# Order of loads and of work at the start of a two-layer decoder kernel

## The chip, the core and the metric

The kernel runs on one core of one Trainium2 chip, as a single launch. TensorE (PE) multiplies, VectorE (DVE), ScalarE (ACT) and GpSimd (POOL) do the element-wise work, and SyncE (SP) only issues transfers between the chip's memory and the on-chip buffers. Each engine takes its own instructions strictly in order and waits on semaphores for the others. The metric is device time in microseconds (us) of one execution; lower is better.

## The reference

Two layers on a sequence of 1024 rows of 1024 numbers. What matters here is how a layer begins:

```python
cos, sin = rope_tables(positions)          # once, used by both layers
cond = jax.nn.silu(c)
# in each layer:
mod = cond @ w_ada + b_ada
shift, scale, gate = jnp.split(mod, 3, axis=-1)
h = layer_norm(x) * (1.0 + scale[:, None, :]) + shift[:, None, :]
proj = h @ w_in
u, v, z_a, q, k, val, z_b, q_idx, k_idx, w_idx = jnp.split(proj, SPLIT_POINTS, axis=-1)
k = apply_rope(k, cos, sin); k_idx = apply_rope(k_idx, cos, sin)
q_idx = apply_rope(q_idx, cq, sq)          # 8 index heads; then scores, top-k, attention
```

Nothing of `h` exists before the shift and scale of its channels do, so at the start of layer 0 the 8 MB of `w_ada` for shift and scale, the rows `x` and the key weights all have to arrive before the first projections can end. Layer 1 finds its own modulation computed during layer 0.

## The kernel before

Rows are tiled by 128 (8 blocks), channels by 128 (8 groups, `NK`), the sequence in two halves of 512 columns. All matrix products are made of three matmuls (high by high, high by low part, low by high), so each weight tile and each column of `h` is split in two: ScalarE rounds the high part, GpSimd or VectorE subtracts the low one (`split`, L310).

`head` (L819) does layer 0's start. It issues the loads in the order of its loop: `x` blocks at positions `XK`, the key weights (`load_kv`) at position `H0`, the rotary tables at `RT`, and 16 pairs of `w_ada` tiles (8 channel groups for each of two column halves c; a pair holds shift and scale columns, tile name `h`). `ada_cols` (L857) forms shift with TensorE (matmul into `po`) and scale with VectorE (a chain of 8 multiply-adds into `ga`), turns both into columns with small matmuls, and VectorE writes four channels of shift and scale to `modT` (L876). The modulated, transposed rows are built by `hT` (L268): TensorE transposes a block of 128 channels (L281), ScalarE scales and shifts it out of PSUM (L288, tile `gc` or `gb`), VectorE casts the high part (L292), and VectorE or GpSimd subtracts the low one (L295, tile `h`). `project_k` (L355) issues the matmuls (L358) into `pacc`.

The order of the work around the change: `head` returns after the first half's key projections and after both halves of `h`; `layer` then alternates between the keys (`kv`, L381) and the first pair of index queries (`queries`, L416). So TensorE's program order is keys of half 0, index queries of half 0, keys of half 1, index queries of half 1, then the second pair of index queries, which is the first work on weights loaded by `layer` itself. Keys share their two PSUM banks (`acc`) with the queries. The rotary tables go through a table in the chip's memory: `rope_tables` (L144) computes four pieces of 32 rows, writes them (L168), and `load_tables` (L170) reads them back four times over, at the start of each layer.

The instruction order inside an engine is not the source order: a list scheduler of the compiler (`schedule_with_timeline_sim=True`) orders each engine's queue by its own estimate of when things are ready. `issue_after` keeps an instruction behind a marked one. SP's queue carries all transfers. Three loads put single 4-byte elements into a column per partition: the condition `c` (L116), the bias of `w_ada` (L180) and `v_norm_g` (L468).

Of the kernel before, what the change touches and what calls it, by code (L numbers as in the profile page):

```python
# [66 lines left out]
class Trunk:  # L67
# [44 lines left out]
    def consts(self):  # L112
        nc, a = self.nc, self.a
        self.cond = self.col("cond", 1, NK)
        cT = self.col("cT", 1, NK)
# [4 lines left out]
        make_identity(nc, self.ident)  # L120
        self.mhalf = self.col("mhalf", 1)
# [14 lines left out]
        self.cs_dram = dram("cs_tab", [2, 32, S])  # L136
# [7 lines left out]
    def rope_tables(self):  # L144
        nc, a = self.nc, self.a
        W = S // 4
        nc.sync.dma_start(self.invf, a["inv_freq"])
        nc.sync.dma_start(self.ztab, a["ztab"][:, 0:36].rearrange("p (k g) -> p k g", k=6))
        nc.sync.dma_start(self.iota8, a["ztab"][:, 36:44])
        pi = self.g("ga", dt=I32)[:, :W]  # L150
        for c in range(4):
            nc.sync.dma_start(pi[c * 32:(c + 1) * 32], a["positions"][0, c * W:(c + 1) * W].partition_broadcast(32))
        ang, kk = self.g("ga")[:, :W], self.g("ga")[:, :W]
        nc.vector.tensor_copy(ang, pi)
        nc.vector.tensor_scalar(ang, ang, self.invf[:, 0:1], None, op0=ALU.mult)
        nc.vector.tensor_scalar(kk, ang, 1.0 / TWO_PI, MAGIC, op0=ALU.mult, op1=ALU.add)
        nc.vector.tensor_scalar(kk, kk, MAGIC, None, op0=ALU.subtract)
        for part in two_pi_parts():
            nc.vector.scalar_tensor_tensor(ang, kk, -part, ang, op0=ALU.mult, op1=ALU.add)
        nc.vector.tensor_scalar(ang, ang, 3.1415925, -3.1415925, op0=ALU.min, op1=ALU.max)  # L160
        sin, cos = self.g("ga")[:, :W], self.g("ga")[:, :W]
        nc.scalar.activation(sin, ang, AF.Sin)
        nc.scalar.activation(cos, ang, AF.Sin, scale=0.5)
        nc.vector.tensor_tensor(cos, cos, cos, op=ALU.mult)
        nc.vector.tensor_scalar(cos, cos, -2.0, 1.0, op0=ALU.mult, op1=ALU.add)
        for w, tab in enumerate((cos, sin)):
            for c in range(4):
                nc.sync.dma_start(self.cs_dram[w][:, c * W:(c + 1) * W], tab[c * 32:(c + 1) * 32])  # L168

    def load_tables(self):  # L170
        self.cos, self.sin = self.u("r"), self.u("r")
        for w, tab in enumerate((self.cos, self.sin)):
            for c in range(4):
                self.nc.sync.dma_start(tab[c * 32:(c + 1) * 32], self.cs_dram[w])


    def ada_begin(self, l):
        self.mod[l] = self.col("modT", 2, 2 * NK)
        bT = self.col("badaT", 2, 2 * NK)
# [74 lines left out]
    NORM = 2  # L254
# [47 lines left out]
    XT = ('r', 'r', 'q', 'q')  # L302
# [33 lines left out]
    def load_kv(self, l):  # L336
# [4 lines left out]
        nc.sync.dma_start(r2, w_in[l, :, C_KI:C_KI + 72].rearrange("(k p) c -> p k c", p=P))  # L341
        hi = [self.u("w", (P, NK, P), F32R) for _ in range(2)]
# [4 lines left out]
        return hi, lo  # L347

# [32 lines left out]
    def kv(self, l, wts, ready=None):  # L381
# [73 lines left out]
    def sgu_setup(self, l):  # L455
# [11 lines left out]
        self.vg = self.col("vg", 1, 4)  # L467
        nc.sync.dma_start(self.vg, a["v_norm_g"][l].rearrange("(j p) -> p j", p=P), allow_slow_non_contiguous=True)  # L468
# [338 lines left out]
    def run(self):  # L807
# [8 lines left out]
        for l in range(DEPTH):  # L816
            wts = self.layer(l, wts if l else self.head())

    def head(self):  # L819
        nc = self.nc  # L820
        xs, raw = [], ([], [])
        for n in range(2 * NK + 1):
            for _ in range(self.XK.count(n)):
                xs.append(self.load_row(self.xin[0], len(xs), ("q", "q", "kd", "kd")[len(xs)]))
            if n == self.H0:
                kvw = self.load_kv(0)
            if n == self.RT:
                self.rope_tables()
            if n == 1:
                self.ada_begin(0)  # L830
            if n < 2 * NK:
                c, k = divmod(n, NK)
# [7 lines left out]
        for x in xs:  # L840
            self.ln_row(x, 4)
        hT = self.hT(0, range(4), xs, *self.HK[0])
        kv = [self.p("acc") for _ in range(2)]
        for c in range(2):
            if c:
                self.ada_cols(c, raw[c])
            for k in range(4 * c, 4 * c + 4):
# [3 lines left out]
        xs = [self.ln_row(self.load_row(self.xin[0], b, self.XT[b - 4])) for b in range(4, NB)]  # L851
        if not self.QE:
            qiw = self.load_pair(0, C_QI, True, "ya")
        self.load_tables()
        self.drain(self.hT(0, range(4, NB), xs, *self.HK[1]))
        return kvw, qiw, kv

    def ada_cols(self, c, tiles):
# [3 lines left out]
        for k, w in enumerate(tiles):  # L862
# [4 lines left out]
            else:  # L867
                nc.vector.scalar_tensor_tensor(sc, w[:, 1, :], ck, sc, op0=ALU.mult, op1=ALU.add)
# [207 lines left out]
```

## Time and profile before

| what | value |
|---|---|
| median of 3 runs (lowest, highest) | 1181.41 us (1180.64, 1185.3) |
| the profiled execution: its time, its span | 1184.14 us, 1182.4 us |
| busy share of the span: PE, DVE, ACT, POOL | 94%, 71%, 43%, 49% |
| chain that ended last, by engine | PE 53%, DVE 8%, DMA 3% |
| projections (L358): matmuls, busy | 2304, 542.5 us |
| mean granted TensorE clock | 0.977 |

The profile has several views. The busy table by stretches gives for each stretch its length and for each engine (PE, its weight loads, DVE, ACT, POOL) the busy time with its number of instructions, then the granted TensorE clock (1.00 is full speed), the mean busy share of the 16 DMA engines, and the GB/s that they moved. The timeline gives start, duration, engine, source line, operation and its tiles (written<-read), how many instructions are merged, and in brackets the idle time before them with what ended it. The table of DMA issues gives the tiles, how many transfers, KB each, and the median us from issue to landing. In the rows, `SPq` is SP's queue of transfers. The first 6 us of the span have no matmul at all, and TensorE's busy share in 40 slices of 30 us starts with 5 and 8 tenths, against 9 in most others.

### The profile page before, as it was taken

Reading aid. Unit: us, or ns where it says so; the run is one execution under the profiler, and the core shown is the slowest. Engines: PE = TensorE matmul, PEld = TensorE weight load, DVE = VectorE, ACT = ScalarE, POOL = GpSimd, SP = SyncE. Lnnn points to the kernel's source line nnn. Section 1 sums busy time; section 2 is a strip of 40 time slices with the busy share of each in tenths; the row PEclk is TensorE's granted clock in tenths of the full one; section 3 lists DMA queues with packets and bytes.
Section 4 is the critical chain, followed back from the end, with each engine's and each line's share of the span. In section 5 each row is a group of like instructions: output and inputs, shape, how many; then the busy total and the mean of one; then the engine's idle time right before and its main releaser. Section 6 shows DMA issues by size and latency. Waiting matters only on the chain.

```text
span 1182.4 us, 16568 instructions
## 1 busy us (share of the span) xinstructions
PE 1109.5 (94%) x5460; PEld 883.6 (75%) x5460; DVE 838.2 (71%) x1884; ACT 512.2 (43%) x988; POOL 575.8 (49%) x485
## 2 busy tenths in 40 slices
PE   5889999999989799989988999999999989999997
PEld 0468888777768688867666788888778877787885
DVE  6775757889869356689975447579985737878775
ACT  0343555221122445466764526552222146667561
POOL 1464311566432666365766532114654457565653
PEclk9989999999989799999998999999999999999999
DMA  8935420378742664331322453213724345132311
GB/s 260 286 94 160 142 72 26 127 244 237 228 130 81 204 188 143 108 99 63 99 89 73 116 152 121 58 57 114 249 90 152 98 141 198 54 102 78 117 36 63
DMA packets 127057, 152.11 MB, mean 129 GB/s; under 512 B 17396, under 2 KB 94580, under 8 KB 126968
## 3 DMA queue, kind: packets, MB, share of 16 engines
q1 hardware_dynamic: 126968, 151.03, 40.5%
q8 instruction: 43, 0.70, 0.2%
q14 instruction: 46, 0.38, 0.1%
HBM read 111.40 MB, written 35.40 MB: 124 GB/s over the span
## 4 chain that ended last, share of the span: by engine, by line
PE 53%; DVE 8%; DMA 3%; issue 2%; POOL 2%; ACT 1%; SPq 0%; DVEq 0%; ACTq 0%; POOLq 0%
PE pacc L358 22%; PE pacc L747 14%; PE ps L685 4%; PE ppt L705 4%; PE po L711 3%; PE po L710 2%; PE ppt L535 2%; PE ps L535 1%; POOL h L732 1%; DVE ga L709 1%; DVE ya L686 1%; DVE w L686 1%; PE po L451 1%; DMA gc<-ya 1%; DVE gb L717 1%
## 5 line engine op out<-in xcount | busy, mean ns | idle before, releaser
L358 PE MATMUL pacc<-h,w 128*128 128x512 f32 (+2 forms) x2304 | 542.5, 389 | 6.9 <-ACT gc L501 6.4
L358 PEld LDWEIGHTS pacc<-h,w 128*128 128x128 f32 (+1 forms) x2304 | 420.0, 187 | 103.0 <-ACT gc L501 10.1
L312 POOL TENSOR_TENSOR w<-wr,w 128x512 fp32r<-128x512 f32 (+1 forms) x100 | 135.0, 1366 | 211.7 <-ACT w L311 203.0
L747 PE MATMUL pacc<-h,gc 128*128 128x512 f32 x768 | 199.6, 405 | 13.4 <-ACT gc L311 12.1
L747 PEld LDWEIGHTS pacc<-h,gc 128*128 128x128 f32 x768 | 145.1, 194 | 43.3 <-ACT gc L311 13.0
L542 DVE SCALAR_TENSOR_TENSOR sc<-gc,wi,sc 128x384 f32<-128x384 f32 (+3 forms) x140 | 97.4, 740 | 56.6 <-ACT gc L537 54.0
L311 ACT ACTIVATE w<-wr 128x512 fp32r<-128x512 f32 (+1 forms) x100 | 56.8, 602 | 154.4 <-PE pacc L358 95.0
L709 DVE TENSOR_TENSOR ga<-ppt,ga 128x512 fp32r<-128x512 f32 x144 | 97.0, 684 | 20.7 <-ACT ga L708 20.1
L685 PE MATMUL ps<-kd,q 128*128 128x512 f32 (+4 forms) x384 | 104.1, 368 | 7.1 <-DVE mx L686 6.5
L708 ACT ACTIVATE ga<-ppt 128x512 fp32r<-128x512 f32 x144 | 82.7, 592 | 38.6 <-PE ppt L705 37.9
L377 POOL TENSOR_TENSOR ga<-ga,ga 128x512 fp32r<-128x512 f32 (+2 forms) x40 | 52.7, 1324 | 83.6 <-ACT ga L376 80.4
L685 PEld LDWEIGHTS ps<-kd,q 128*128 128x128 f32 x384 | 64.2, 192 | 23.8 <-DVE mx L686 17.4
L694 POOL TENSOR_SCALAR w<-w,rd 128x256 f32<-128x256 f32 (+6 forms) x77 | 61.4, 801 | 40.8 <-DVE rd L693 24.4
L691 ACT ACTIVATE w<-w,mx 128x256 f32<-128x256 f32 (+6 forms) x77 | 60.6, 787 | 35.5 <-DVE mx L686 34.9
L705 PE MATMUL ppt<-ident,w 128*128 128x128 f32 x349 | 74.1, 275 | 0.5 <-POOL w L694 0.5
L248 POOL TENSOR_TENSOR rs<-rs,mhalf 128x1 f32<-128x1 f32 x48 | 30.2, 638 | 86.4 <-DVE rs L247 85.8
L710 PE MATMUL po<-ga,vv 128*128 128x512 f32 x144 | 61.9, 430 | 9.1 <-DVE gb L717 5.7
L550 DVE TENSOR_SCALAR_CACHE_REDUCE junkd<-sc,sv 128x384 int8<-128x384 f32 (+2 forms) x72 | 67.8, 942 | 1.7
L711 PE MATMUL po<-ga,vv 128*128 128x512 f32 x144 | 63.1, 438 | 4.1 <-DVE ga L709 3.9
L694 POOL TENSOR_SCALAR ya<-ya,rd 128x256 f32<-128x256 f32 (+6 forms) x51 | 40.8, 801 | 52.3 <-DVE rd L693 30.4
L537 ACT ACTIVATE gc<-ppt 128x384 f32<-128x384 f32 (+3 forms) x96 | 47.8, 526 | 40.2 <-PE ppt L535 35.8
L705 PE MATMUL ppt<-ident,ya 128*128 128x128 f32 x227 | 58.0, 275 | 1.4 <-DVE modT L235 1.4
(197 smaller groups left out, 1729.9 us busy)
## 6 DMA issues: line engine op xcount, KB each, us to landing
wr<-in_w_in SPq DMA_DIRECT2D x50, 512.0 KB, 4.4
r<-in_w_ada SPq DMA_DIRECT2D x32, 512.0 KB, 4.7
q<-q SPq DMA_DIRECT2D x112, 128.0 KB, 3.2
q<-ga SPq DMA_DIRECT2D x48, 256.0 KB, 2.2
h<-in_w_ada SPq DMA_DIRECT2D x32, 256.0 KB, 4.8
wr<-in_w_out SPq DMA_DIRECT2D x16, 512.0 KB, 4.1
r<-r SPq DMA_DIRECT2D x14, 512.0 KB, 3.6
r<-x SPq DMA_DIRECT2D x12, 512.0 KB, 4.5
```

Source lines behind the costliest of these rows:

```text
L312: self.nc.gpsimd.tensor_tensor(lo, src, hi.bitcast(F32), op=ALU.subtract)
L358: self.nc.tensor.matmul(acc[:m, :tn], w[:, k, :m], h[:, k % 2, t0:t0 + tn], start=(k == 0 and i == 0), stop=(k == NK - 1 and i == 2))
L542: nc.vector.scalar_tensor_tensor(sc[:, c0:c0 + w], r[:, :w], wsc, sc[:, c0:c0 + w], op0=ALU.mult, op1=ALU.add)
L550: self.nc.vector.tensor_scalar(j[:, :n], sc, thr, None, op0=op, op1=ALU.add, accum_out=out)
L685: self.last_pe = nc.tensor.matmul(ps[:, :w], q[:, g * 4 + h, :], self.KD[x][:, c0:c0 + w], start=(x == 0), stop=(x == 1)).ins
L694: nc.gpsimd.tensor_scalar(pm[:, :n], pm[:, :n], rd, 0.0, op0=ALU.mult, op1=ALU.add)
L705: nc.tensor.transpose(pt[:, h * P:(h + 1) * P], pr[h][:, kt * P:(kt + 1) * P], self.ident)
L708: nc.scalar.activation(ph, pt, AF.Copy)
L709: nc.vector.tensor_tensor(pl, pt, ph.bitcast(F32), op=ALU.subtract)
L710: nc.tensor.matmul(o, self.V[:, kt, :], ph, start=(kt == 0), stop=False)
L711: nc.tensor.matmul(o, self.V[:, kt, :], pl, start=False, stop=(kt == i))
L747: self.nc.tensor.matmul(acc, s[:, k, :], m[:, cs], start=(first and k == i == 0), stop=(not more and k == 3 and i == 2))
```

## The change

- `c`, the `w_ada` bias and `v_norm_g` are loaded as rows (8, 16 and 4 rows of 128) and turned into columns by one TensorE transpose each (`ada_bias` for the bias).
- SP's order at the start is fixed by the source: `c`, the bias, the eight 512 KB tiles of column half 0 (shift and scale in one transfer, 2 KB runs as before), `x` blocks 0 to 3, key weights, the eight tiles of column half 1, `x` blocks 4 to 7 (before: two of these stood behind the first table reads), the first index weights. The small inputs of the rotary tables are issued from ScalarE's queue.
- The rotary table operations on VectorE start behind the last sum of column half 0 (`mark["sum"]`), the table is written as 128 rows of 1 KB in 2 transfers instead of 8, behind the last `w_ada` load; the reads are 8 as before, in 1 KB runs instead of 4 KB.
- `NORM = 6`: the eight normalisations of layer 0's `x` blocks move from VectorE to ScalarE (L262's form), with one more small VectorE operation each.
- `head` becomes a generator: keys of half 0, then, in the same pass, `h` and keys of half 1, and only then the index queries of both halves. `load_pair` and `load_kv` are split into load and split parts.

```diff
 def consts(self):
-        nc.sync.dma_start(cT, a["c"].rearrange("o (k p) -> p (o k)", p=P), allow_slow_non_contiguous=True)
-        nc.scalar.activation(self.cond, cT, AF.Silu)
+        crow = self.g("gb", (NK, P))
+        nc.sync.dma_start(crow, a["c"].rearrange("o (k p) -> (o k) p", p=P))
...
+        nc.tensor.transpose(cT[:, :NK], crow, self.ident[:NK, :NK])
+        nc.scalar.activation(self.cond, cT[:, :NK], AF.Silu)
...
+    def rope_inputs(self):
...
+        nc.scalar.dma_start(self.invf, a["inv_freq"])
...
+    def rope_tables(self, pi, dma):
...
+        with self.behind("sum"):
+            nc.vector.tensor_copy(ang, pi)
...
-            for c in range(4):
-                nc.sync.dma_start(self.cs_dram[w][:, c * W:(c + 1) * W], tab[c * 32:(c + 1) * 32])
+            with self.tc.issue_after(dma):
+                nc.sync.dma_start(self.cs_dram[w], tab)
...
+        self.brow = self.t("brow", [2 * NK, P])
+        self.nc.sync.dma_start(self.brow, self.a["b_ada"][l, 0:2 * D].rearrange("(k p) -> k p", p=P))
+
+    def ada_bias(self, l):
...
-        self.nc.sync.dma_start(bT, self.a["b_ada"][l, 0:2 * D].rearrange("(k p) -> p k", p=P), allow_slow_non_contiguous=True)
-        self.nc.vector.tensor_scalar(bT[:, NK:], bT[:, NK:], 1.0, None, op0=ALU.add)
+        nc.tensor.transpose(pt[:, :2 * NK], self.brow, self.ident[:2 * NK, :2 * NK])
+        nc.vector.tensor_copy(self.bT[:, :NK], pt[:, :NK])
+        nc.vector.tensor_scalar(self.bT[:, NK:], pt[:, NK:2 * NK], 1.0, None, op0=ALU.add)
...
-    NORM = 2
+    NORM = 6
...
 def head(self):
+        ada_loads(0)
+        pi = self.rope_inputs()
+        xs = [self.load_row(x, b, ("q", "q", "kd", "kd")[b]) for b in range(4)]
+        kvr = self.kv_raw(0)
+        dma = ada_loads(1)
+        xs += [self.load_row(x, b, "r") for b in range(4, NB)]
+        qir = self.pair_raw(0, C_QI)
+        self.ada_bias(0)
         self.ada_cols(0, raw[0])
+        for b in range(4):
+            self.ln_row(xs[b], 4)
+        self.rope_tables(pi, dma)
+        kvw = self.kv_split(*kvr)
+        out = {}
+        for half in range(2):
+            hT = self.hT(0, range(half * 4, half * 4 + 4), xs[half * 4:half * 4 + 4], *self.HK[half])
+            kv = [self.p("acc") for _ in range(2)]
+            for k in range(NK):
+                if half == 0 and k == 4:
+                    self.ada_cols(1, raw[1])
                 next(hT)
                 for j in range(2):
-                    self.project_k(kv[j], kvw[0][j], kvw[1][j], 0, k, (P, 72)[j])
+                    self.project_k(kv[j], kvw[0][j], kvw[1][j], half, k, (P, 72)[j])
+            out[half] = kv
+            if half == 0:
+                for b in range(4, NB):
+                    self.ln_row(xs[b], 4)
+                self.load_tables()
+            else:
+                qiw = self.pair_split(qir, True, "ya")
+            yield kvw, qiw if half else None, out
...
 def layer(self, l, wts):
-        first = [self.kv(l, wts[0], *wts[2:]), self.queries(l, 1, 0, wts[1])]
-        for _ in range(2):
-            for g in first:
-                next(g)
-                ada_step(self.ADA0)
+        kvg = self.kv(l, wts[0], wts[2])
+        if head:
+            next(kvg)
+            wts = next(head)
+            next(kvg)
+        qg = self.queries(l, 1, 0, wts[1])
+        for r in range(2):
+            if not head:
+                next(kvg)
+            next(qg)
```

What stands on VectorE around the second `modT` (the shift and scale of channels 512 to 1023), before. `r_441` and `r_452` are `x` blocks 4 and 5.

```order
L868 SCALAR_TENSOR_TENSOR ga_353<-h_206,cond_61,ga_353 128x512
L868 SCALAR_TENSOR_TENSOR ga_353<-h_209,cond_61,ga_353 128x512
L868 SCALAR_TENSOR_TENSOR ga_353<-h_212,cond_61,ga_353 128x512
L243 BN_STATS bn_443<-r_441 128x6 x2
L245 BN_AGGR mv_446<-bn_443 128x2
L243 BN_STATS bn_454<-r_452 128x6 x2
L247 TENSOR_SCALAR rs_448<-mv_446 128x1
L876 TENSOR_TENSOR modT_106<-ps_370,badaT_107 128x2x4
L245 BN_AGGR mv_457<-bn_454 128x2
L247 TENSOR_SCALAR rs_459<-mv_457 128x1
L252 TENSOR_SCALAR r_441<-r_441,mv_446,rs_448 128x1024
```

And now; `r_161` and `r_163` are `x` blocks 6 and 7, and the eight sums of column half 1 stand ahead of these rows.

```order
L257 BN_STATS bn_467<-r_161 128x6 x2
L259 BN_AGGR mv_459<-bn_456 128x2
L261 TENSOR_SCALAR rs_450<-mv_448 128x1
L257 BN_STATS bn_478<-r_163 128x6 x2
L259 BN_AGGR mv_470<-bn_467 128x2
L261 TENSOR_SCALAR rs_461<-mv_459 128x1
L275 TENSOR_SCALAR nmb_453<-mv_448,rs_450 128x1
L259 BN_AGGR mv_481<-bn_478 128x2
L261 TENSOR_SCALAR rs_472<-mv_470 128x1
L261 TENSOR_SCALAR rs_483<-mv_481 128x1
L275 TENSOR_SCALAR nmb_464<-mv_459,rs_461 128x1
L912 TENSOR_TENSOR modT_169<-ps_374,badaT_170 128x2x4
```

The `modT` write stood behind the statistics of two `x` blocks and now stands behind those of all four.

ScalarE from the second column half's shift row to the evacuations (L288) that use the second `modT`, and on to the first key evacuation (L396); before:

```order
L872 ACTIVATE ga_352<-po_351 1x512
L288 ACTIVATE gc_382<-ppt_381,modT_106 128x512
L288 ACTIVATE gb_397<-ppt_396,modT_106 128x512
L288 ACTIVATE gc_412<-ppt_411,modT_106 128x512
L288 ACTIVATE gc_427<-ppt_426,modT_106 128x512
L311 ACTIVATE ya_489<-wr_485 128x512
L311 ACTIVATE ya_495<-wr_485 128x512
L311 ACTIVATE ya_489<-wr_487 128x512
L311 ACTIVATE ya_495<-wr_487 128x512
L396 ACTIVATE gb_601<-pacc_281 64x512
```

Now, from the normalisation of `x` block 4 to the last evacuation of half 0 (L302 is the line L288 before; `wr_165` and `wr_167` are the first index weights, each 512 KB):

```order
L276 ACTIVATE r_157<-r_157,nmb_453,rs_450 128x1024
L324 ACTIVATE ya_687<-wr_165 128x512
L276 ACTIVATE r_159<-r_159,nmb_464,rs_461 128x1024
L302 ACTIVATE gc_386<-ppt_385,modT_169 128x512
L302 ACTIVATE gb_401<-ppt_400,modT_169 128x512
L302 ACTIVATE gc_416<-ppt_415,modT_169 128x512
L276 ACTIVATE r_161<-r_161,nmb_475,rs_472 128x1024
L324 ACTIVATE ya_693<-wr_165 128x512
L324 ACTIVATE ya_687<-wr_167 128x512
L324 ACTIVATE ya_693<-wr_167 128x512
L276 ACTIVATE r_163<-r_163,nmb_486,rs_483 128x1024
L302 ACTIVATE gc_431<-ppt_430,modT_169 128x512
```

The four evacuations of half 0 stood together; now four normalisations of 1024 columns and four weight splits, which need two later loads, stand ahead of or between them.

TensorE at the end of the keys of half 0 (`pacc_281`, `pacc_282`), before; `ya_489` is the first index weight:

```order
L358 MATMUL pacc_281<-h_286,w_181 128x512
L358 MATMUL pacc_282<-h_286,w_182 72x512
L358 MATMUL pacc_281<-h_290,w_181 128x512
L358 MATMUL pacc_281<-h_286,w_183 128x512
L358 MATMUL pacc_282<-h_290,w_182 72x512
L358 MATMUL pacc_282<-h_286,w_184 72x512
L358 MATMUL pacc_651<-h_283,ya_489 128x256
L358 MATMUL pacc_651<-h_287,ya_489 128x256
```

And now (`pacc_285`, `pacc_286`; L382 is the line L358 before):

```order
L382 MATMUL pacc_285<-h_290,w_269 128x512
L382 MATMUL pacc_286<-h_290,w_270 72x512
L382 MATMUL pacc_285<-h_294,w_269 128x512
L382 MATMUL pacc_285<-h_290,w_271 128x512
L382 MATMUL pacc_286<-h_294,w_270 72x512
L382 MATMUL pacc_286<-h_290,w_272 72x512
L432 MATMUL ppt_545<-ident_65,gb_507 128x64
L295 MATMUL ppt_567<-ident_65,r_157 128x128
L295 MATMUL ppt_567<-ident_65,r_159 128x128
L295 MATMUL ppt_567<-ident_65,r_161 128x128
L295 MATMUL ppt_567<-ident_65,r_163 128x128
```

The index queries of half 0 followed the keys of half 0; now the transposes for half 1 follow (`r_157` to `r_163`), with its keys behind them.

## Rows read from the trace of the kernel before

**Rows 1.** Busy table by stretches, the first 52 us.
```profile
6.00:8.00 2.00, 1.73 (x2) 0.11 (x2) 1.04 (x5) 0.00 (x0) 0.00 (x0) 1.00 0.91 119
8.00:10.00 2.00, 1.30 (x3) 0.09 (x2) 0.82 (x2) 0.00 (x0) 0.56 (x1) 1.00 0.63 184
10.00:12.00 2.00, 1.53 (x4) 0.50 (x3) 0.23 (x2) 0.00 (x0) 0.00 (x0) 1.00 0.36 99
12.00:28.00 16.00, 10.77 (x18) 1.38 (x18) 13.43 (x31) 1.13 (x3) 1.95 (x2) 1.00 1.00 340
28.00:36.00 8.00, 6.77 (x34) 3.14 (x34) 6.47 (x14) 4.19 (x9) 2.23 (x3) 1.00 0.92 276
36.00:48.00 12.00, 12.00 (x46) 5.28 (x45) 11.18 (x13) 1.25 (x4) 6.47 (x6) 1.00 1.03 348
48.00:52.00 4.00, 2.93 (x23) 2.24 (x22) 2.96 (x11) 2.79 (x4) 1.54 (x2) 1.00 0.58 58
```
**Rows 2.** DMA issues of the first 60 us.
```profile
badaT<-in_b_ada SPq DMA_DIRECT2D x2, 8.0 KB, 4.3
```
**Rows 3.** DMA issues from 51 to 59.5 us.
```profile
wr<-in_w_in SPq DMA_DIRECT2D x3, 512.0 KB, 3.4
```
**Rows 4.** Timeline of DVE around the second modT.
```profile
46.82 1.29 DVE L243 BATCH_NORM_STATS2 bn<-r 128x6 f32<-128x512 f32 x2 [0.62 <-DMA r<-in_x]
...
48.67 0.17 DVE L876 TENSOR_TENSOR modT<-ps,badaT 128x8 f32<-128x8 f32 x1 [0.51 <-PE ps L874]
```
**Rows 5.** Timeline of ACT, from the second modT to the first key evacuations.
```profile
48.87 0.78 ACT L288 ACTIVATE gc<-ppt,modT 128x512 f32<-128x512 f32 x1 [0.87 <-DVE modT L876]
...
55.75 1.15 ACT L311 ACTIVATE ya<-wr 128x512 fp32r<-128x512 f32 x2 [4.09 <-DMA wr<-in_w_in]
...
59.23 0.59 ACT L396 ACTIVATE gb<-pacc 64x512 f32<-64x512 f32 x1
```
**Rows 6.** Groups by form on ACT: busy, mean ns | idle time and its releaser.
```profile
L262 ACT ACTIVATE r<-r,nmb,rs 128x1024 f32<-128x1024 f32 x13 | 16.1, 1241 | 4.2 <-DVE nmb L261 4.2
```
**Rows 7.** Timeline of PE, projections from 52 to 120 us.
```profile
52.66 5.38 PE L358 MATMUL pacc<-h,w 128*128 128x512 f32 x22 [0.50 <-DVE h L295]
...
60.49 4.34 PE L358 MATMUL pacc<-h,ya 128*128 128x256 f32 x34 [2.46 <-ACT ga L366]
...
78.44 9.51 PE L358 MATMUL pacc<-h,w 128*128 128x512 f32 x40
...
89.72 4.81 PE L358 MATMUL pacc<-h,ya 128*128 128x512 f32 x20 [0.34 <-ACT ga L366]
...
95.69 6.66 PE L358 MATMUL pacc<-h,ya 128*128 128x512 f32 x28
...
102.19 18.11 PE L358 MATMUL pacc<-h,w 128*128 128x256 f32 x101
```
**Rows 8.** Timeline of all engines, 63 to 71 us.
```profile
63.12 1.79 POOL L312 TENSOR_TENSOR w<-wr,w 128x512 fp32r<-128x512 f32 x1 [0.19 <-ACT w L311]
63.69 1.76 DVE L369 TENSOR_TENSOR ga<-ga,r 64x512 f32<-64x512 f32 x1
...
65.45 0.67 DVE L371 TENSOR_TENSOR ga<-ga,r 64x512 f32<-64x512 f32 x1
...
70.55 0.76 ACT L288 ACTIVATE gc<-ppt,modT 128x512 f32<-128x512 f32 x1
```
**Rows 9.** Busy table, two stretches of the second half's keys.
```profile
69.00:78.00 9.00, 7.96 (x29) 5.39 (x30) 6.85 (x10) 4.66 (x10) 5.97 (x4) 0.62 0.33 82
...
88.00:89.70 1.70, 0.27 (x1) 0.13 (x1) 0.00 (x0) 1.63 (x4) 1.70 (x2) 1.00 0.78 205
```
**Rows 10.** Busy table, two later stretches.
```profile
100.00:130.00 30.00, 30.00 (x159) 26.16 (x158) 17.53 (x22) 10.64 (x22) 12.86 (x11) 1.00 0.55 170
...
240.00:280.00 40.00, 40.00 (x231) 31.83 (x230) 35.60 (x65) 10.16 (x18) 24.92 (x18) 1.00 0.80 263
```

More of the change, by code (lines that the diff above doesn't have):

```diff
@@ L228, in ada_mod @@
         nc = self.nc
+        if grp == 0:
+            with self.behind("pe"):
+                self.ada_bias(l)
         for c in range(2):
@@ L334, in load_pair, with kv_raw @@
         return hi, lo
-    def load_kv(self, l):
+    def load_pair(self, l, c0, rope, tag="w"):
+        return self.pair_split(self.pair_raw(l, c0), rope, tag)
+    def kv_raw(self, l):
         nc, w_in = self.nc, self.a["w_in"]
@@ L341, in load_kv, with kv_split @@
         nc.sync.dma_start(r2, w_in[l, :, C_KI:C_KI + 72].rearrange("(k p) c -> p k c", p=P))
+        return r1, r2
+    def kv_split(self, r1, r2):
         hi = [self.u("w", (P, NK, P), F32R) for _ in range(2)]
@@ L347, in load_kv @@
         return hi, lo
+    def load_kv(self, l):
+        return self.kv_split(*self.kv_raw(l))
     def project(self, hi, lo, half, m=P, t0=0, tn=HALF):
@@ L379, in rope, with kv @@
         return out
-    def kv(self, l, wts, ready=None):
+    def kv(self, l, wts, ready):
         nc = self.nc
@@ L389, in kv @@
             t0 = half * HALF
-            if ready and half == 0:
-                pa, pb = ready
+            if half in ready:
+                pa, pb = ready[half]
             else:
@@ L473, in sgu_setup @@
             nc.sync.dma_start(self.bsum[g * 64:(g + 1) * 64], a["b_spatial"][l].rearrange("(j g) t -> g j t", g=2)[g].partition_broadcast(64))
+        self.vg = self.col("vg", 1, 4)
+        pt = self.p("pt")
+        nc.tensor.transpose(pt[:, :4], vrow, self.ident[:4, :4])
+        nc.vector.tensor_copy(self.vg, pt[:, :4])
         mx = self.sgu_mm(vb)
@@ L816, in run @@
         for l in range(DEPTH):
-            wts = self.layer(l, wts if l else self.head())
+            wts = self.layer(l, wts if l else None)
     def head(self):
[L820 to L832, printed above, removed]
+        nc, x = self.nc, self.xin[0]
@@ L833, in head, with ada_loads @@
+        self.ada_begin(0)
+        w_ada = self.a["w_ada"][0, :, 0:2 * D].rearrange("(k p) (g c n) -> k p g c n", p=P, g=2, c=2)
+        raw = ([], [])
+        def ada_loads(c):
+            for k in range(NK):
                 w = self.u("h", (P, 2, 512))
-                for grp in range(2):
-                    nc.sync.dma_start(w[:, grp, :], self.a["w_ada"][0, k * P:(k + 1) * P, grp * D + c * 512:grp * D + (c + 1) * 512])
+                ins = nc.sync.dma_start(w, w_ada[k][:, :, c, :]).ins
@@ L836, in head @@
                 raw[c].append(w)
-        if self.QE:
-            qiw = self.load_pair(0, C_QI, True, "ya")
-        self.ada_cols(0, raw[0])
[L840 to L847, printed above, removed]
+            return ins
+        ada_loads(0)
+        pi = self.rope_inputs()
@@ new lines, in head @@
+        xs = [self.load_row(x, b, ("q", "q", "kd", "kd")[b]) for b in range(4)]
[4 more added lines that the diff above has]
+        self.ada_bias(0)
+        self.ada_cols(0, raw[0])
+        for b in range(4):
[6 more added lines that the diff above has]
+            kv = [self.p("acc") for _ in range(2)]
+            for k in range(NK):
+                if half == 0 and k == 4:
+                    self.ada_cols(1, raw[1])
@@ L867, in ada_cols @@
             else:
-                nc.vector.scalar_tensor_tensor(sc, w[:, 1, :], ck, sc, op0=ALU.mult, op1=ALU.add)
+                ins = nc.vector.scalar_tensor_tensor(sc, w[:, 1, :], ck, sc, op0=ALU.mult, op1=ALU.add).ins
+        if c == 0:
+            self.mark["sum"] = ins
         pm = self.p("s")
@@ L886, in layer @@
         last = l + 1 == DEPTH
+        head = None if l else self.head()
         if l:
             self.load_tables()
+            wts = (*wts, {})
+        else:
+            wts = next(head)
         self.ya = []
@@ L908, in ada_step @@
                     k -= 1
-        first = [self.kv(l, wts[0], *wts[2:]), self.queries(l, 1, 0, wts[1])]
-        for _ in range(2):
-            for g in first:
-                next(g)
-                ada_step(self.ADA0)
+        kvg = self.kv(l, wts[0], wts[2])
+        if head:
+            next(kvg)
+            wts = next(head)
+            next(kvg)
[4 more added lines that the diff above has]
+            next(qg)
         masks = {0: self.mask3[:, P:], 1: self.mask3}
```

47 lines of the change are left out of this document (19 added, 28 removed).

## The prediction

> **What bounds the kernel now.** I read three views in this order: the busy table by stretches, to see whether a microsecond won at the start is kept; the same table of the first 52 us, to see what the start waits for; and the timelines of the engines there, to see which queue ends last. In the later stretches TensorE is busy for 30.00 of 30 and 40.00 of 40 us [rows 10]: from 102 to 280 us it runs without a gap, so what arrives earlier there leaves earlier. The reader should see the opposite at the start: the DMA engines are the bound up to 48 us (busy share 0.92 to 1.03), but they move 340 and 348 GB/s in good stretches, 119, 184 and 99 GB/s between 6 and 12 us, and 58 GB/s between 48 and 52 us [rows 1]. In both bad stretches the loads of single 4-byte elements are in flight: `badaT` has 8 KB and takes 4.3 us to land, twice [rows 2]. TensorE's key and index projections then run in pieces from 52.66 to 102.19 us [rows 7]; at 102.19 begins the first work on weights that `layer` loads itself. That point is my milestone: everything that `head`, the keys and the first pair of index queries do lies before it in both kernels.
>
> **The change part by part.** All times are on the clock of the profiled execution (1184.14 us, 2.7 above the median of the runs).
>
> *Transfers.* Between 6 and 12 us before moves 2 x (119 + 184 + 99) = 0.80 MB; at 340 GB/s it would be 2.04 MB. The missing 1.24 MB are 3.6 us [rows 1]. The second bad stretch misses 4 x (348 - 58) = 1.16 MB, 3.3 us. Both go: the new loads are 8, 16 and 4 rows. Now the last `x` block that counts. Before, block 5 is the last ahead of the second `modT`; VectorE's wait for it ends at 46.82 [rows 4]. After, blocks 6 and 7 stand ahead too (+1.05 MB), and the table writes (0.26 MB) go behind: +0.79 MB, +2.3 us at 348 GB/s. The table reads (1.05 MB, 3.0 us), which before are in flight beside blocks 4 and 5, also go behind; how much of them ran ahead of block 5 is not visible, so 0 to 3.0 us, and I take the middle. Block 7 lands at 46.8 + 2.3 - 3.6 - 1.5 = 44.0 us (42.5 to 45.5).
>
> *The second `modT`.* It now stands behind the statistics of all four blocks. From block 7's landing: 1.29 for its two statistics, then eight small operations at about 0.17 each, the duration of the `modT` write itself [rows 4]: 44.0 + 1.3 + 1.4 = 46.7. Before, it ended at 48.84. So of the transfers' gain 2.1 us is left here.
>
> *ScalarE to the end of half 0's keys.* Here the new order costs. The first index weight follows block 7 by 0.26 + 0.52 MB, 2.2 us: 46.2. Then ScalarE in its order: split 0.58 (1.15 for two), normalisation 1.24 [rows 6], three evacuations at about 0.7 (0.78 alone), normalisation 1.24, three splits 1.73, normalisation 1.24, last evacuation 0.78 [rows 5]: 46.2 + 8.9 = 55.1. VectorE's cast and subtraction and the last four matmuls (5.38 us for 22, so 0.24 each) add about 2.1: the keys of half 0 end at 57.2, against 52.66 + 5.38 = 58.04 [rows 7]. The gain is down to 0.8 us. The eight normalisations that leave VectorE are thus not free on ScalarE: the first four lie under the loads of the second column half, the last three are in this chain.
>
> *Key evacuations.* Another weight split stands ahead of them on ScalarE. Its load may go out when GpSimd has finished with the first index weight (ScalarE's split of it ends at 51.9, GpSimd's subtraction takes 1.3 to 1.8 [rows 8]: 53.3); a 512 KB weight lands in 3.4 us on a free queue [rows 3], so 56.7, and the split is done at 57.3. It is just hidden. Behind it wait the evacuations and, through them, TensorE. Four of them at 0.61 (59.23 starts the first before, each 0.59 plus its issue [rows 5]) end at 59.8; the first modulated evacuation of half 1 starts there. Before it started at 70.55 [rows 8], since the `x` blocks came late and the index queries of half 0 stood ahead.
>
> *Second half's keys.* Before, from that evacuation to the last key matmul: 70.55 to 78.44 + 9.51 = 87.95 [rows 7, 8], 17.4 us. TensorE alone needs 48 x 0.238 = 11.4 us, plus about 1 for transposes and 3.5 until the first high part is cast (rotary products stand ahead of it on VectorE): 15.9. I take 16.6, between both: 59.8 + 16.6 = 76.4.
>
> *Index queries.* TensorE waits for two banks to be freed (the stretch of 1.70 us with 0.27 us of matmul [rows 9]), taken as 1.5; then half 0 in 256 columns, 48 x 4.34/34 = 6.1, small transposes 1.2, and half 1, 4.81 + 6.66 = 11.5 [rows 7]. The milestone is at 76.4 + 20.3 = 96.7, against 102.19: 5.5 us earlier.
>
> *The rest.* The three added transposes and the table operations behind the first sums lie under the column-half loads (8.4 MB of `w_ada`, 24 us at 348 GB/s); if that cover were gone they would cost about 4 us of VectorE. Fewer table writes: hidden. Layer 1's table reads in 1 KB runs: the weights in Rows 3 have runs of 1 KB too and bring 512 KB in 3.4 us, so a 128 KB read should not be slower; 0, at most 1 us. Layer 1's bias costs one transpose and two small copies, under 0.5 us. The key copies on SP now come in two groups ahead of any index-query copy; the index queries' own copies follow their projections as before. Order changes far behind the head are swaps of neighbours: 0, between -2.5 and 2.5 us.
>
> Sum: -5.5 us. 1184.14 becomes 1178.6; on the median of the runs 1181.41 becomes 1175.9, which I predict. About 5.9 us (0.5%) is what a measurement of this kernel can tell from no change.
>
> [...] Rows 8 show a rotary product of 1.76 us while GpSimd subtracts, and its twin in 0.67 alone: 1.09 us lost. [...]
>
> **The rivals.**
> 1. *The transfers gain more.* All table reads leave the way (block 7 at 42.5: -1.5), the first index weight is there before `modT`, so one split and one normalisation slip under VectorE's statistics (-1.3), and half 1 runs at TensorE's pace (-0.7): -9.0 in all, 1172.4. For it: the engines reached 348 GB/s for 12 us with 256 KB transfers, and these are now 512 KB. Against: 276 GB/s in the stretch with the key weights [rows 1].
> 2. *VectorE and GpSimd take turns throughout half 1.* Six subtractions at 1.3 and fourteen VectorE operations, about 9 us, in single file instead of beside each other: 19.7 us instead of 16.6, so 3.1 lost: 1179.0. To this I add the case that a part of the gain is absorbed later (up to 1181).
> [...]
>
> **How the numbers follow.** Forecast 0.40 (1173 to 1179), rival 1 0.28, rival 2 0.17, rival 3 0.15. Faster by over 0.5% (below 1175.5): nearly all of rival 1 and half of the forecast, 0.46. Slower (above 1187.3): two thirds of rival 3, and a little for what I don't see, 0.12. Within: 0.42. Range 1167 to 1186: to rival 1's end with 5 us more of transfers, and up to rival 3's first figure.
>
> **What would show it.** Right: no stretch of the first 50 us under 250 GB/s after the first transfers; the second `modT` near 46.7 with VectorE waiting for `x` block 7 just before; the last evacuation of half 0 near 55 behind weight splits; the last key matmul of half 1 near 76; the second pair of index queries near 97. Wrong: `modT` at 41 or earlier, or a wait of ScalarE for a weight of 3 us or more ahead of the key evacuations, a granted clock under 0.8 in half 1's keys, or a milestone that moves while the end does not.

## The result: slower, and not at the start

The changed kernel takes 1198.19 us in the median of four runs (1196.24 to 1198.82), the kernel before 1181.03 beside it: ratio 1.0128, 95% interval 1.0096 to 1.016. I forecast 1175.9. The profiled execution took 1196.24 us with a span of 1194.3 us, 11.9 more than before's 1182.4, at the same mean granted clock (0.976 against 0.977).

The head did nearly what the steps said. The busy table by stretches, changed kernel (columns as in [rows 1]):

```profile
6.00:8.00 2.00, 2.00 (x3) 0.21 (x2) 0.77 (x2) 0.00 (x0) 0.00 (x0) 1.00 0.99 343
8.00:10.00 2.00, 1.44 (x4) 0.09 (x2) 0.65 (x1) 0.00 (x0) 0.00 (x0) 1.00 1.07 370
10.00:12.00 2.00, 1.34 (x3) 0.09 (x2) 0.93 (x3) 0.00 (x0) 0.00 (x0) 1.00 1.06 374
12.00:28.00 16.00, 7.75 (x25) 2.22 (x25) 13.91 (x36) 5.36 (x11) 4.94 (x7) 0.81 1.08 373
28.00:36.00 8.00, 8.00 (x31) 3.05 (x31) 7.45 (x14) 5.36 (x7) 3.53 (x5) 0.96 1.05 392
36.00:48.00 12.00, 10.39 (x52) 6.24 (x50) 9.47 (x26) 4.24 (x6) 5.35 (x6) 1.00 0.91 268
```

Between 6 and 48 us no stretch falls under 250 GB/s any more, and 12 to 36 us move more than before (373 and 392 against 340 and 276). The stretch from 48 to 52 us, 58 GB/s before, has 163 now:

```profile
48.00:52.00 4.00, 4.00 (x13) 2.52 (x14) 3.39 (x5) 4.00 (x7) 2.37 (x2) 0.65 0.74 163
```

The timelines of VectorE, ScalarE and TensorE, changed kernel:

```profile
42.80 1.27 DVE L257 BATCH_NORM_STATS2 bn<-r 128x6 f32<-128x512 f32 x2
...
45.51 0.17 DVE L912 TENSOR_TENSOR modT<-ps,badaT 128x8 f32<-128x8 f32 x1 [0.37 <-PE ps L910]
```
```profile
52.96 0.77 ACT L302 ACTIVATE gc<-ppt,modT 128x512 f32<-128x512 f32 x1
56.17 0.63 ACT L324 ACTIVATE w<-wr 128x512 fp32r<-128x512 f32 x1 [2.44 <-DMA wr<-in_w_in]
56.83 0.59 ACT L420 ACTIVATE gb<-pacc 64x512 f32<-64x512 f32 x1
...
59.16 0.76 ACT L302 ACTIVATE gc<-ppt,modT 128x512 f32<-128x512 f32 x1
```
```profile
55.94 1.19 PE L382 MATMUL pacc<-h,w 128*128 128x512 f32 x4 [0.34 <-DVE h L309]
...
70.67 8.16 PE L382 MATMUL pacc<-h,w 128*128 128x512 f32 x34 [0.19 <-DVE h L309]
...
84.54 14.43 PE L382 MATMUL pacc<-h,ya 128*128 128x256 f32 x74
98.81 19.13 PE L382 MATMUL pacc<-h,w 128*128 128x256 f32 x106
```

The milestone, the second pair of index queries, starts at 98.81 against 102.19 [rows 7]: 3.4 us earlier. From there to the end of the span it is 1194.3 - 98.8 = 1095.5 us, against 1182.4 - 102.2 = 1080.2: 15.3 us longer, in work that the change hardly touches. The groups by form show where, before first, then changed:

```profile
L358 PE MATMUL pacc<-h,w 128*128 128x512 f32 x2112 | 510.2, 394 | 6.9 <-ACT gc L501 6.4 <-DVE h L295 0.5
L747 PE MATMUL pacc<-h,gc 128*128 128x512 f32 x768 | 199.6, 405 | 13.4 <-ACT gc L311 12.1 <-POOL gc L312 1.3
```
```profile
L382 PE MATMUL pacc<-h,w 128*128 128x512 f32 x2112 | 522.8, 399 | 8.6 <-ACT gc L529 5.1 <-DVE h L309 3.2 <-DVE h L306 0.3
L775 PE MATMUL pacc<-h,gc 128*128 128x512 f32 x768 | 202.9, 410 | 11.9 <-ACT gc L324 11.8
```

The same 2880 matmuls are busy 12.6 + 3.3 = 15.9 us longer. It is not the clock: in a stretch of layer 1 without any gap at clock 1.00, TensorE starts 112 matmuls before and 109 now (a few records can be missing, so the next number decides):

```profile
930.00:955.00 25.00, 25.00 (x112) 20.72 (x111) 11.10 (x26) 8.05 (x12) 5.73 (x5) 1.00 0.28 95
```
```profile
930.00:955.00 25.00, 25.00 (x109) 20.12 (x108) 15.87 (x33) 4.47 (x8) 6.92 (x6) 1.00 0.16 62
```

From the start times of neighbouring 512-column projections in the trace (some 2,700 pairs; L358 and L747, or the lines that answer to them), the mean interval is 227.9 ns before and 233.2 ns now. With 3,072 such matmuls that is 16.3 us. So the 512-column projections of both layers got slower by 2.3%, and the question was why.

### The profile page after: what moved, and what is told of

The parts are those of the page before. It is cut to its first block, busy times and chain, and to the rows that moved or that the text cites. A ratio compares the mean times of both kernels' runs of the same rounds, so it can differ in the third digit from the quotient of the medians.

```text
span 1194.3 us, 16577 instructions
## 1 busy us (share of the span) xinstructions
PE 1124.2 (94%) x5465; PEld 883.9 (74%) x5465; DVE 832.5 (70%) x1888; ACT 521.9 (44%) x996; POOL 567.1 (47%) x485
## 5 line engine op out<-in xcount | busy, mean ns | idle before, releaser
L382 PE MATMUL pacc<-h,w 128*128 128x512 f32 (+2 forms) x2304 | 554.5, 394 | 8.6 <-ACT gc L529 5.1
L382 PEld LDWEIGHTS pacc<-h,w 128*128 128x128 f32 (+1 forms) x2304 | 420.2, 187 | 117.3 <-ACT gc L529 8.8
L325 POOL TENSOR_TENSOR w<-wr,w 128x512 fp32r<-128x512 f32 (+1 forms) x100 | 131.6, 1332 | 217.4 <-ACT w L324 203.4
L775 PE MATMUL pacc<-h,gc 128*128 128x512 f32 x768 | 202.9, 410 | 11.9 <-ACT gc L324 11.8
L401 POOL TENSOR_TENSOR ga<-ga,ga 128x512 fp32r<-128x512 f32 (+2 forms) x40 | 49.2, 1239 | 90.6 <-ACT ga L400 90.6
L530 POOL TENSOR_TENSOR ya<-ya,gc 128x512 f32<-128x512 f32 x32 | 47.1, 1478 | 26.8 <-ACT gc L529 17.8
L262 POOL TENSOR_TENSOR rs<-rs,mhalf 128x1 f32<-128x1 f32 x48 | 28.1, 598 | 66.4 <-DVE rs L261 65.5
```

Of the source, the lines that this page charges most:

```text
L325: self.nc.gpsimd.tensor_tensor(lo, src, hi.bitcast(F32), op=ALU.subtract)
L382: self.nc.tensor.matmul(acc[:m, :tn], w[:, k, :m], h[:, k % 2, t0:t0 + tn], start=(k == 0 and i == 0), stop=(k == NK - 1 and i == 2))
L775: self.nc.tensor.matmul(acc, s[:, k, :], m[:, cs], start=(first and k == i == 0), stop=(not more and k == 3 and i == 2))
```

## Experiments

**What makes the matmuls slower: addresses.** Tiles get their place in the on-chip buffer in the order in which the program first asks for them. The change asks for new ones (`brow`), drops one (`cT`) and asks for others in another order, so `h` moves from byte 26368 of a partition to 24800 and `w` from 120832 to 152608; the PSUM banks move too. In the next fourteen kernels only empty tiles are added, or tiles reserved ahead, so instructions and their order stay those of the kernel named. First shifts of 32 bytes:

```diff
 # a1: the changed kernel, head()           a2: the second tile alone; a3: the first alone
-        ada_loads(0)
+        self.sb.tile([P, 8], F32, tag="pad0", ...); ada_loads(0); self.sb.tile([P, 8], F32, tag="pad1", ...)
 # b1: the kernel before, consts()
+        self.sb.tile([P, 8], F32, tag="pad0", ...); self.cond = self.col("cond", 1, NK)
```

> The changed kernel, with one empty tile of 32 bytes ahead of the tiles h and one behind them: h starts at a multiple of 64 bytes again (as in the kernel before), every other tile keeps its place modulo 64 bytes. The instructions and their order are those of the changed kernel. Theory A (the start address of the operand that streams through TensorE decides: 512-column matmuls start every 233 ns instead of 227 since h starts 32 bytes beside a multiple of 64): the interval is 227 ns again, about 3000 matmuls of 512 columns on h are 6 ns shorter each, some 17 us: 1181 us (1177 to 1183). Rival B (the address of the weights held in the array, tiles w, ya, gc, decides): 233 ns, 1198 us. Rival C (not the addresses in the on-chip buffer but the PSUM banks, the order of the work or the chip): 233 ns, 1198 us.

> The changed kernel, with one empty tile of 32 bytes behind the tiles h: h stays 32 bytes beside a multiple of 64, all tiles behind it (ga, q, kd, wr, r, w, gc, ya) come to multiples of 64. Theory A: projections at 233 ns still; only matmuls that stream ga, kd or r may gain a little, 1195 to 1199 us. Rival B: 227 ns, 1181 us. Rival C: 233 ns, 1198 us.

> The changed kernel, with one empty tile of 32 bytes ahead of the tiles h: h and all large tiles behind it come to multiples of 64 bytes. It is the change without its shift of addresses. Theory A: 227 ns; the head's gain of 3.4 us at the start of the second pair of index queries is then left: 1176 to 1181 us. Rival B: 227 ns too, the same time. Rival C: 233 ns, 1198 us.

> The kernel before, with one empty tile of 32 bytes ahead of everything: every tile moves by 32 bytes, nothing else changes. Theory A and rival B: the 512-column matmuls of the projections start every 233 ns, 1196 to 1200 us. Rival C: 227 ns, 1181 us.

Measured: ratios 1.0146 (1.0093 to 1.0199), 1.0141 (1.0085 to 1.0196), 1.0115 (1.0057 to 1.0174) and, for the shifted kernel before, 1.0023 (0.9997 to 1.0049). Theory A and rival B both fall: no single tile's place modulo 64 does it. Rival C stood, so next the PSUM banks, and all places together:

```diff
 # p1: the changed kernel with PSUM in before's order (p2: the kernel before, the other way round)
+        [self.ps.tile([P, 512], F32, tag=t, bufs=self.PBUFS[t], ...) for t in ("o", "s", "acc", "pt")]
 # s1: the changed kernel, places in before's order; s2: both lines
+        [self.sb.tile([P, w], F32, tag=t, bufs=..., ...) for t, w in dict(cond=8, ..., q=1024, h=1024, ...).items()]
```

> The changed kernel with the four kinds of PSUM tile reserved in the order of the kernel before: the projections' sums (acc) lie in banks 3 and 4 again instead of 6 and 7, s in 1 and 2, pt in 5 to 7, o in 0. Instructions, order and addresses in the other buffer as in the changed kernel. Theory C1 (the PSUM banks decide the interval of the 512-column matmuls): 227 ns, 1176 to 1181 us. Rival C2 (the place in the on-chip buffer of h against w and the other large tiles, beyond what the 32-byte shifts moved): 233 ns, 1196 us. Rival C3 (neither: the instructions themselves): 233 ns, 1196 us.

> The kernel before with its PSUM tiles in the banks of the changed kernel: acc in 6 and 7, s in 0 and 1, pt in 2 to 4, o in 5. Theory C1: 233 ns, 1196 us. Rivals C2 and C3: 227 ns, 1181 us.

> The changed kernel with the tiles of the on-chip buffer reserved in the order of the kernel before, so that q, h, ga, kd, wr, w, gc, gb, r, ya and vv have its addresses byte for byte; PSUM as in the changed kernel. Theory C1: 233 ns, 1196 us. Rival C2: 227 ns, 1176 to 1181 us. Rival C3: 233 ns, 1196 us.

> Both of the above in one: the changed kernel's instructions with all addresses of the kernel before, in the on-chip buffer and in PSUM. Theories C1 and C2: 227 ns and 1176 to 1181 us, which is then what the change of order is worth without the move of its tiles. Rival C3: 233 ns, 1196 us.

Measured: 1.0125 (1.0095 to 1.0156), 1.0002 (0.9981 to 1.0023), 1.0007 (0.998 to 1.0033), 1.0018 (0.9998 to 1.0037). The banks do nothing (C1 falls, p1 stays at 233.2 ns, p2 at 228.0); the places restored bring 228.0 ns back (C2), though not the 1176 to 1181 us expected with it (s1 takes 1183.12, s2 1183.54). The changed kernel with them, groups by form:

```profile
L382 PE MATMUL pacc<-h,w 128*128 128x512 f32 x2112 | 510.3, 393 | 8.1 <-DVE h L309 5.4 <-ACT gc L529 2.5 <-DVE h L306 0.3
```

In the kernels so far the interval follows one number, the distance between the streamed operand `h` and the stationary weights (`w`, `gc`, `ya`, alike modulo 256). Three kernels set it on purpose, by one empty tile behind `h`:

```diff
 # d1: 16 words, d2: 48 words, in the changed kernel; d3: 16 words in the kernel before
+        ada_loads(0); self.sb.tile([P, 48], F32, tag="pad", ...)
```

> The changed kernel with an empty tile of 64 bytes between h and the tiles behind it: the distance from the weights (w, gc, ya) to h, which was 192 modulo 256 bytes, becomes 128. In the runs so far the interval of the 512-column matmuls goes with this distance: 0 modulo 256 (before, before shifted, places as before): 227 ns; 192: 233 ns; 160: 234.5 ns. Theory D128 (the distance modulo 128 decides, and 0 is the fast one): 227 ns, 1178 to 1184 us. Rival D256 (modulo 256): 230 to 236 ns, 1190 to 1200 us. Rival L (not the distance in small, but in which larger part of the buffer the tiles lie, w at 120 to 145 KB before and 152 to 177 KB now): 233 ns, 1196 us.

> The changed kernel with an empty tile of 192 bytes behind h: the distance from the weights to h becomes 0 modulo 1024 bytes for w and gc and 512 for ya; everything else stays where the change put it. Theory D128 and rival D256: 227 ns, 1178 to 1184 us. Rival L: 233 ns, 1196 us.

> The kernel before with an empty tile of 64 bytes behind h, nothing else changed: the distance from the weights to h becomes 192 modulo 256 bytes (64 modulo 128), as in the changed kernel. Theory D128 and rival D256: 233 ns, 1195 to 1200 us. Rival L: 227 ns, 1181 us.

Measured: d1 1.0121 (1.0072 to 1.0169), d2 1.0029 (1.0008 to 1.005), d3 1.0102 (1.0055 to 1.0149). D256 holds in all three by the interval; the times of d2 (1185.24 us) and d3 (1193.24) lie 1 to 2 us outside of those expected. d3 is the cleanest: the kernel before, with nothing but 64 empty bytes, loses 11 us, and its projections look like those of the changed one:

```profile
L358 PE MATMUL pacc<-h,w 128*128 128x512 f32 x2112 | 521.5, 399 | 4.5 <-ACT gc L501 4.3 <-POOL w L312 0.2
```

Three single runs fill in the other distances (32, 40 and 24 words in d2's line):

> The changed kernel with 128 bytes between h and the tiles behind it: distance from the weights to h 64 modulo 256. Theory D256 says only that it isn't 227 ns: 229 to 235 ns. If the interval grows with the distance from 0 on either side (d1 at 128 had 232, 160 had 234, 192 had 233): about 230 ns, 1188 to 1193 us. Rival (only multiples of 128 matter, the rest is alike): 233 ns, 1196 us.

> The same with 160 bytes: distance 32 modulo 256. If the interval grows with the distance from 0: 227 to 229 ns, 1183 to 1188 us. Rival: 233 ns, 1196 us.

> The same with 96 bytes: distance 96 modulo 256. If the interval grows with the distance from 0: 231 ns, 1190 to 1195 us. Rival: 233 ns, 1196 us.

Measured: 1187.05, 1195.59 and 1198.19 us, with one run of before at 1184.9. All kernels together:

| distance h - w modulo 256 | kernels | mean interval, ns |
|---|---|---|
| 0 | before, b1, p2, s1, s2, d2 | 227.9 to 228.0 |
| 32 | g32 | 233.1 |
| 64 | g64 | 229.4 |
| 96 | g96 | 233.3 |
| 128 | d1 | 232.5 |
| 160 | a1, a2 | 234.0 |
| 192 | changed, a3, p1, d3 | 233.2 |

The cost does not grow with the distance, as I had guessed for g32 (227 to 229): 0 is best, 64 nearly as good, the rest alike. In these kernels all tiles behind `h` move together, so its distance to the weights isn't separated from its distance to the other tiles there.

**What the change is worth without it.** With the addresses (s1, s2) or the distance (d2) restored it is between equal and 0.3% slower, not 0.5% faster. Four kernels at the addresses of before take the change apart:

```diff
 # n1: normalisations back on VectorE
-    NORM = 6
+    NORM = 2
 # n2: index queries of half 0 between the keys again (n3: n1 and n2)
-                for j in range(2):
+                for j in range(2 - 2 * half):          # head: no keys of half 1
...
-            next(kvg)
-            wts = next(head)
-            next(kvg)
+            wts = next(head)
         for r in range(2):
+            next(kvg)
             next(qg)
 # n4: the kernel before with the row loads of c, both biases and v_norm_g alone
-        nc.sync.dma_start(cT, a["c"].rearrange("o (k p) -> p (o k)", p=P), allow_slow_non_contiguous=True)
+        nc.sync.dma_start(crow, a["c"].rearrange("o (k p) -> (o k) p", p=P))
+        nc.tensor.transpose(cT[:, :NK], crow, self.ident[:NK, :NK])
```

> The changed kernel with the addresses of the kernel before, and the eight normalisations of layer 0 back on VectorE (NORM = 2). With the addresses restored the change took 1183 us against 1182 of before, where 1176 was forecast. Theory E1 (the normalisations in ScalarE's chain eat the gain of the transfers): 1178 to 1180 us. Rival E2 (the keys of both halves ahead of the index queries cost it): 1183 to 1186, since VectorE gets 8 times 0.7 to 1.1 us back. Rival E3 (the transfers bring less than the trace suggests): 1183 us.

> The changed kernel with the addresses of before, and TensorE's order of before: keys of half 0, index queries of half 0, keys of half 1, index queries of half 1; loads, tables and normalisations as changed. Theory E2: 1178 to 1180 us. Rival E1: 1183 to 1186 us (the index weights' splits and half 1's evacuations come earlier in ScalarE's queue). Rival E3: 1183 us.

> Both of the above: of the change only the loads, the tables and the order of SP's queue are left, at the addresses of before. If E1 or E2 holds: 1176 to 1180 us, the gain of the transfers alone (my steps give 3.6 us of bad stretch and 2.3 us later x blocks: second modT 2 us earlier). E3: 1181 to 1183 us.

> The kernel before with the row loads and transposes of c, of both biases and of v_norm_g alone, at the addresses of before; order of loads, tables, normalisations and keys as before. My steps: the two bad stretches cost 3.6 and 3.3 us of transfers; the first lies ahead of x block 5 and of the second modT: about 3 us earlier at the second index pair, 1178 to 1179 us. Rival E3 (in the timed runs the 4-byte loads cost less, or what waits for them has room): 1180 to 1182 us.

Measured, each against the same runs of before (1181.57 us): n1 1184.17 us, 1.0015 (0.9993 to 1.0038); n2 **1176.14 us, 0.9954 (0.9937 to 0.9972)**; n3 1178.27 us, 0.9973 (0.9955 to 0.9991); n4 1182.57 us, 1.001 (0.9991 to 1.0029). E2 holds and E1 falls (n2 came out below the 1178 to 1180 us expected; n4 missed the 1178 to 1179 us of my steps and lies a little above E3's range). The keys of both halves ahead of the index queries cost 1.0007 - 0.9954 = 0.5%, 6 us (s1 and n2 were timed at different times, each against its own runs of before); n1 and n3, timed together, differ in this order alone, 1184.17 against 1178.27 us, which is 5.9 us; the normalisations on ScalarE gain some 2 us in n2's order (interval ends overlap) and nothing in the other. n2 is the best version, faster than both kernels.

What the order costs at the milestone shows between 60 and 69 us. Busy table by stretches, s1 (the change at the addresses of before), then n2:

```profile
60.00:69.00 9.00, 5.73 (x30) 3.69 (x28) 9.00 (x12) 5.20 (x9) 6.64 (x5) 1.00 0.17 44
```
```profile
60.00:69.00 9.00, 8.76 (x62) 8.08 (x63) 8.95 (x11) 6.74 (x13) 5.54 (x5) 1.00 0.03 8
```

In both VectorE is busy all the time: it makes the high parts that half 1's keys wait for. In n2 TensorE works on index queries meanwhile, which need only half 0. Timeline of TensorE, s1, then n2:

```profile
65.66 3.04 PE L382 MATMUL pacc<-h,w 128*128 128x512 f32 x12 [2.70 <-DVE h L309]
70.45 8.14 PE L382 MATMUL pacc<-h,w 128*128 128x512 f32 x34 [1.75 <-DVE h L309]
...
98.52 5.67 PE L382 MATMUL pacc<-h,w 128*128 128x256 f32 x46
```

```profile
60.24 3.14 PE L382 MATMUL pacc<-h,ya 128*128 128x256 f32 x24 [0.34 <-ACT ga L390]
64.53 3.13 PE L382 MATMUL pacc<-h,ya 128*128 128x256 f32 x24
67.50 6.35 PE L382 MATMUL pacc<-h,w 128*128 128x512 f32 x27
74.37 5.12 PE L382 MATMUL pacc<-h,w 128*128 128x512 f32 x21 [0.53 <-DVE h L309]
...
92.14 8.10 PE L382 MATMUL pacc<-h,w 128*128 128x256 f32 x56
```

n2's milestone is at 92.14, s1's at 98.52. The keys of half 1 end at 70.45 + 8.14 = 78.6 in s1 and at 74.37 + 5.12 = 79.5 in n2: they gain 0.9 us from going first, and 2 x 3.13 us of queries come behind them.

n4, without the 4-byte loads, gains no time. Its rates in the two bad stretches of [rows 1] rise from 119 to 234 and from 58 to 294 GB/s:

```profile
6.00:8.00 2.00, 2.00 (x4) 0.26 (x3) 1.25 (x5) 0.00 (x0) 0.56 (x1) 1.00 0.85 234
...
48.00:52.00 4.00, 2.93 (x21) 2.10 (x20) 3.69 (x9) 3.16 (x5) 1.90 (x2) 1.00 0.93 294
```

Half 1's first modulated evacuation then starts at 69.09 us against 70.55 [rows 8], yet the milestone is at 102.69 against 102.19 and the time the same. Timelines of ScalarE and TensorE, n4:

```profile
69.09 0.76 ACT L299 ACTIVATE gc<-ppt,modT 128x512 f32<-128x512 f32 x1
```
```profile
102.69 17.50 PE L369 MATMUL pacc<-h,w 128*128 128x256 f32 x99
```

Between them TensorE has a lower granted clock than before. Busy table by stretches, before, then n4:

```profile
69.00:80.00 11.00, 9.96 (x40) 6.90 (x41) 8.80 (x16) 6.66 (x12) 6.06 (x5) 0.69 0.34 85
```
```profile
69.00:80.00 11.00, 10.09 (x33) 7.01 (x34) 8.94 (x15) 6.03 (x10) 5.58 (x5) 0.53 0.38 94
```

The difference, 0.16 of 11 us or 1.8 us at full clock, is about what was lost there (an estimate from these two rows). So n4 shows that the time does not notice these loads, not that nothing waited for them; and one execution of each kernel can't tell, since kernels with before's loads start half 1 anywhere from 69.40 (d3) to 73.21 us (b1). In n2 and n3 the clock in this stretch is 1.00, so n3's 0.27% may be in part the clock.

## Why the prediction was wrong

**The step that failed** is the last one, "The rest": I put everything far behind the head at 0, between -2.5 and 2.5 us. It was +15.3 us, and the 512-column matmuls alone are busy 15.9 us longer. Ahead of it a gain of 5.5 us was forecast and 3.4 came. My own sign of being wrong, a milestone that moves while the end does not, is what happened. The order of instructions there is the same but for neighbours, and I took that for the same work. The places of the operands are part of the work, and the diff had shown both causes of their move: new tiles, and a new order of first use. None of the three rivals held it. The upper end of my range, 1186, takes rival 3's first figure, a low granted clock throughout half 1's keys; that was my estimate, and no run shows this term. In the changed kernel the granted clock in these keys, 59 to 79 us, is 0.91 where I had named less than 0.8, and s1, at clock 1.00 from 60 to 69 us, ends them within 0.3 us of the changed kernel.

**Transfers**: about right in size. The first bad stretch went and the second shrank, and the statistics of the `x` blocks then ran without waiting for a transfer (the last pair starts at 42.8 us and ends at 44.1; I had block 7 landing at 44.0). But the row loads alone leave the time where it was (n4); loads, tables and SP's order together bring 0.27% (n3).

**Second `modT`**: forecast to end at 46.7, measured 45.51 + 0.17 = 45.7, but its wait is for TensorE's small transposes and not for `x` block 7's statistics.

**ScalarE to the end of half 0's keys**: 55.1 and 57.2 forecast; the last evacuation ends at 53.7, the keys at 55.94 + 1.19 = 57.1. **Key evacuations**: the split of the next weight 57.3 forecast, 56.8 measured, and half 1's first evacuation 59.8 against 59.16. Here the order read together with the trace gave each point within 1.5 us.

**Second half's keys**: 16.6 us forecast, 78.83 - 59.16 = 19.7 measured, which is rival 2's figure. Three VectorE operations of kinds that run in 0.67 or 0.41 us alone (the other two rows) are long beside operations on GpSimd (timelines of VectorE and GpSimd, changed kernel):

```profile
60.50 0.67 DVE L396 TENSOR_TENSOR ga<-ga,r 64x512 f32<-64x512 f32 x1
...
61.44 1.76 DVE L394 TENSOR_TENSOR ga<-ga,ga 64x512 f32<-64x512 f32 x1
63.13 0.41 DVE L306 CAST h<-gc 128x512 fp32r<-128x512 f32 x1
...
64.06 1.75 DVE L309 TENSOR_TENSOR h<-gc,h 128x512 fp32r<-128x512 f32 x1
65.74 1.49 DVE L306 CAST h<-gc 128x512 fp32r<-128x512 f32 x1
```
```profile
61.19 1.47 POOL L325 TENSOR_TENSOR w<-wr,w 128x512 fp32r<-128x512 f32 x1 [3.04 <-DVE ga L396]
63.67 1.59 POOL L309 TENSOR_TENSOR h<-gc,h 128x512 fp32r<-128x512 f32 x1 [1.01 <-PE ps L295]
65.23 1.72 POOL L401 TENSOR_TENSOR ga<-ga,ga 64x512 fp32r<-64x512 f32 x1
```

In each of these three pairs the VectorE operation ends 0.3 to 0.6 us behind the GpSimd one beside it. Whether such pairs make up the whole of the 3.1 us was not tested.

**Index queries**: 20.3 forecast, 98.81 - 78.83 = 20.0 measured. The term was right, but I never priced the alternative. In the kernel before, half 0's share of it lay inside the wait for half 1; in n2 the same loads and normalisations with that order reach the milestone 6.4 us before s1.

**Left open.** In their profiled executions s1, s2 and d2 reach the milestone 1.7 to 3.7 us ahead of before (102.19), and in the timed runs they gain nothing. An odd execution of before does not explain it: other kernels with its order reach the milestone at 102.69 (p2), 103.26 (d3) and 104.95 us (b1). What the record does show is that a lead at the milestone need not reach the end. I took from [rows 10] that what arrives earlier leaves earlier, and that holds to 280 us only; from there to 340 us TensorE has idle time. Busy table by stretches, s1, then n2:

```profile
280.00:340.00 60.00, 57.51 (x242) 45.36 (x241) 52.47 (x124) 14.56 (x24) 36.56 (x24) 0.97 0.69 208
```
```profile
280.00:340.00 60.00, 53.54 (x219) 41.60 (x218) 48.32 (x114) 12.81 (x21) 29.82 (x22) 0.94 0.62 186
```

n2 leads s1 by 6.4 us at the milestone, and the two profiled executions end 0.5 us apart (spans 1175.7 and 1176.2 us). So the 7 us between their medians (1176.14 and 1183.12) rest on the timed runs, and no trace follows them to the end. The granted clock may be part of it: its mean is 0.974 over the ten runs of s1 and 0.977 over the 25 of before beside them, and among the runs of s1 the fastest have the higher clock (1177.61 us at 0.978, 1186.64 at 0.973). Whether the clock takes the gain, or waits behind the milestone lower the clock, was not tested.

## What to carry to other kernels

When a change adds, drops or reorders tiles, compare the addresses of the hot operands before and after, as well as the order of instructions (here the addresses took a 512-column projection from 227.9 to 233.2 ns); reserving the hot tiles first, in a fixed order, takes this off the table, and one empty tile of a few bytes tests it. Compare the busy time of a group that the change doesn't touch, at equal clock, before looking for waits. Work that fills a wait is free where it stands: before moving a chain ahead of it, price the wait that stays empty (5.9 us here, n1 against n3). A milestone near the start checks the steps before it; look for the next idle time behind it before counting its lead as time won.

## What the runs showed that I had not expected

In these kernels the start-to-start interval of a 512-column matmul on 4-byte operands at clock 1.00 depends on the distance of its two operands in the on-chip buffer modulo 256 bytes: 226.8 ns in the steady part at 0 (the means above hold the first few of each chain), 233.3 at 192; shifting both by 32 bytes (b1) does nothing (227.9 to 228.0 ns, as before). It holds for the projections and output products, but not for the 96 projections whose weights have only 72 columns (a mean of 232 ns in both kernels). The 256-column projections are slightly the other way, a median of 120 ns at distance 0 and 114 in the changed kernel, and the index scores, whose two operands lie at distance 0 in d2, stayed at a median of 231 ns there against 227 before. So the distance is not the whole rule, and why the array cares was not settled.
